# A NaN-ignoring row maximum: the first small tile becomes a group of its own

## The chip, the core and the metric

The kernel runs on one core of one Trainium2 chip. The metric is the device time of one execution in microseconds (us); the median of three runs is given. A core has several engines that work side by side and wait for one another through semaphores. Four are used here: DVE (vector engine), ACT (scalar engine), POOL (GpSimd) and SP, which only issues the transfers. Sixteen DMA engines carry out those transfers between HBM, the main memory, and SBUF, the on-chip memory with its 128 partitions.

## The reference

The input has 32 x 2048 = 65,536 rows of 2048 floats, with one value in ten NaN. For each row the largest value that is not NaN is wanted.

```python
def reference(x: np.ndarray, axis: int) -> np.ndarray:
    return np.nanmax(x, axis=axis).astype(np.float32)
```

The input is 536.87 MB, the output 0.26 MB. Every input byte is read once.

## The kernel before

**Groups and tiles.** The rows are cut into groups, and each group is spread over the 128 partitions: with s rows per partition, partition p holds the s rows from row p x s of the group on. In memory the step from one partition to the next is therefore s x 8 KB. L299 makes this view for the loads and L300 the same for the results. A group is worked through in tiles, each of them some rows of every partition. `TILES` (L16 on) lists 74 of them. Tile 0 has one row per partition (1 MB in all), each of tiles 1 to 73 has seven (7168 KB), so the tiles hold 512 rows per partition. `GROUPS` (L50) cuts the list into groups of 15, 15, 15, 15, 13 and 1 tiles, that is 99, 105, 105, 105, 91 and 7 rows per partition.

**One tile.** An entry of `TILES` has three lists in quarter rows (512 floats): how the tile is cut into loads, into pieces for ACT and POOL, and into reduces for DVE. Most tiles are one load of 56 KB per partition, three pieces and two reduces. The last dozen tiles are cut ever finer. Loads are issued on SP (L316). ACT then reads the upper 16 bits of each float and writes a 16-bit key in which every NaN has become a very low value (L235, written to one of three key buffers `kt`). POOL turns the key back into the upper half of a float, in place in the tile (L245); for a part of the pieces ACT does that instead. DVE takes the maximum of each row (L252).

**What sets the order.** The program writes its order out by hand. A small class, `Order`, gives each instruction the semaphore waits that it needs, and each engine carries out its instructions in the order in which they are written. There are three tile buffers `xt`: the load of a tile waits for the last reduce of the tile three before it. So at any time the queue of SP holds about two loads. All loads go through that one queue.

**Results.** The row maxima of groups 0 to 3 are gathered in a buffer `acc`, those of the last two in a part of a small buffer `lead`. `LATE` (L54) names the first group that goes to the second buffer. A row that has only NaN shows up as a particular very low value; two instructions over all maxima of a buffer (`find`, L258 and L272) look for it and turn it into NaN. `FLAGGED` (L53) says behind which groups DVE does so: behind group 3 for groups 0 to 3 together, and behind group 5 for that group. For group 4 POOL does it, as its last work. The stores of the results, one per group, are issued on SP behind the last load (L460 on); each waits for the check of its group.

Of the kernel before, what the change touches and what calls it, by code (L numbers as in the profile page):

```python
# [15 lines left out]
TILES = (  # L16
    [([4], [4], [4])]
    + [([28], [7, 9, 12], [16, 12])] * 7
    + [([28], [9, 12, -7], [8, 20])]
    + [([28], [7, 9, 12], [16, 12])] * 7  # L20
    + [([28], [9, 12, -7], [8, 20])]
    + [([28], [7, 9, 12], [16, 12])] * 7
    + [([28], [9, 12, -7], [8, 20])]
    + [([28], [7, 9, 12], [16, 12])] * 7
# [23 lines left out]
)  # L48

GROUPS = [TILES[i : i + 15] for i in range(0, 60, 15)] + [TILES[60:73], TILES[73:]]  # L50


FLAGGED = (3, 5)  # L53
LATE = 4  # L54

APART = (70, 71, 72, 73)
WIDE = 7
# [115 lines left out]
def kernel(  # L173
# [28 lines left out]
    of = out.bitcast(i32).flatten_outer_dims().rearrange("r c -> (r c)")  # L202
    rows = [sum(sum(loads) for loads, _, _ in g) * Q // D for g in GROUPS]
    assert R == P * sum(rows)
# [5 lines left out]

    early = sum(rows[:LATE])
    lead = sing.tile([P, LEAD // 4], f32, name="lead")
    acc1 = lead[:, : sum(rows[LATE:])]
    late = lead[:, LEAD // 4 - 1 - rows[LATE] : LEAD // 4 - 1].bitcast(i32)
    warm = lead[:, LEAD // 4 - 1 :]
# [5 lines left out]
    def maxima(lo, hi):  # L221

        if hi <= early:
            return acc0[:, lo:hi]
        assert lo >= early
        return acc1[:, lo - early : hi - early]

    with tc.tile_critical():  # L228
# [25 lines left out]
        def find(who, engine, deps, acc, none, op):  # L254
            e = order.add(
                who,
                engine,
                lambda: engine.tensor_scalar(  # L258
                    out=none,
                    in0=acc,  # L260
                    scalar1=NONE,
                    scalar2=float(0x00800000),
                    op0=ALU.is_equal,
                    op1=ALU.mult,
                ),
                deps,
            )
            bits = acc.bitcast(i32)
            return order.add(
                who,  # L270
                engine,
                lambda: engine.tensor_tensor(  # L272
                    out=bits, in0=bits, in1=none, op=op
                ),
                [e],
            )
# [20 lines left out]
        r0 = 0  # L297
        for gi, (s, g) in enumerate(zip(rows, GROUPS)):
            xg = xr[r0 : r0 + P * s].rearrange("(p s) d -> p (s d)", p=P)  # L299
# [144 lines left out]
            stores.append((og, acc.bitcast(i32)))  # L444
            if gi == LATE:
                late_after = after
            elif gi not in FLAGGED:
                continue
            lo, flagged = flagged, first + s
            if gi == LATE:  # L450
                late_acc = maxima(lo, flagged)
            else:
# [3 lines left out]
                ready += [e] * (gi + 1 - len(ready))  # L456
            if gi == len(GROUPS) - 1:
                e = find("pool", nc.gpsimd, late_after, late_acc, late, ALU.add)
                ready[LATE] = e
        for (og, bits), e in zip(stores, ready):  # L460
# [46 lines left out]
```

## Time and profile before

| | before |
|---|---|
| time, median of 3 runs | 1252.76 us (1252.72 to 1252.77) |
| span of the profiled execution | 1251.6 us |
| its own time beside the span | not given apart; the median is 1.2 us above the span |
| busy: DVE, ACT, POOL | 1110.8, 965.6, 1168.5 us |
| DMA, mean over the span | 429 GB/s |
| a load of one tile, issue to landing (median) | 22.6 us |

The span runs from the first to the last instruction on the core. A busy time is the sum of an engine's instructions. In the lines of the groups and the timeline, "out<-in" names the buffers, a number with "x" behind it counts instructions, and what stands in brackets is the idle time ahead of the instruction and what ended it. "SPq" is the queue on which SP issues transfers. Tiles are counted from 0 in this text.

### The profile page before, as it was taken

Reading aid. Unit: us, or ns where it says so; the run is one execution under the profiler, and the core shown is the slowest. Engines: PE = TensorE matmul, PEld = TensorE weight load, DVE = VectorE, ACT = ScalarE, POOL = GpSimd, SP = SyncE. Lnnn points to the kernel's source line nnn. Section 1 sums busy time; section 2 is a strip of 40 time slices with the busy share of each in tenths; the row PEclk is TensorE's granted clock in tenths of the full one; section 3 lists DMA queues with packets and bytes.
Section 4 is the critical chain, followed back from the end, with each engine's and each line's share of the span. In section 5 each row is a group of like instructions: output and inputs, shape, how many; then the busy total and the mean of one; then the engine's idle time right before and its main releaser. Section 6 shows DMA issues by size and latency. Waiting matters only on the chain.

```text
span 1251.6 us, 893 instructions
## 1 busy us (share of the span) xinstructions
DVE 1110.8 (89%) x181; ACT 965.6 (77%) x273; POOL 1168.5 (93%) x242
## 2 busy tenths in 40 slices
DVE  0888989888889888898988888988888899999999
ACT  3777887778777877788777877777777778999997
POOL 2999989998999899998999899999999999989998
DMA  9999999999999999999999999999999999999997
GB/s 415 440 411 440 440 433 418 440 440 440 431 420 440 440 438 431 422 440 440 438 433 420 440 440 438 434 418 440 440 438 435 420 438 436 425 438 429 429 427 299
DMA packets 15991, 537.20 MB, mean 429 GB/s; under 512 B 2544, under 2 KB 2544, under 8 KB 3568
## 3 DMA queue, kind: packets, MB, share of 16 engines
q1 hardware_dynamic: 15984, 537.14, 99.4%
q14 instruction: 7, 0.06, 0.0%
HBM read 536.87 MB, written 0.26 MB: 429 GB/s over the span
## 4 chain that ended last, share of the span: by engine, by line
DMA 40%; DVE 29%; POOL 21%; ACT 8%; issue 1%; SPq 0%
DMA xt<-in_x_dram 40%; DVE acc L252 21%; POOL xt L245 21%; ACT kt L235 8%; DVE lead L252 7%; ACT xt L235 1%; SPq L316 0%; DVE none L258 0%; DVE lead L272 0%; SPq L502 0%; SPq L228 0%
## 5 line engine op out<-in xcount | busy, mean ns | idle before, releaser
L245 POOL TENSOR_SCALAR xt<-kt 128x3584 int16<-128x3584 uint16 (+11 forms) x236 | 1167.4, 4946 | 78.3 <-ACT kt L235 64.9
L235 ACT ACTIVATE kt<-xt 128x3584 uint16<-128x3584 int16 (+9 forms) x247 | 913.4, 3734 | 278.7 <-DMA xt<-in_x_dram 258.6
L252 DVE TENSOR_REDUCE acc<-xt 128x3 f32<-128x6144 f32 (+3 forms) x119 | 896.2, 7570 | 136.1 <-POOL xt L245 128.6
L252 DVE TENSOR_REDUCE lead<-xt 128x1 f32<-128x2048 f32 (+4 forms) x56 | 211.4, 3848 | 1.0 <-POOL xt L245 0.9
L235 ACT ACTIVATE xt<-kt 128x512 int16<-128x512 uint16 (+6 forms) x24 | 52.9, 2204 | 0.7
L235 ACT ACT_TABLE_LOAD x1 | 1.3, 1283 | 0.9 <-SPq L228 0.9
L252 DVE TENSOR_REDUCE xt<-xt 128x1 f32<-128x1536 f32 x1 | 1.7, 1741 | 0.0
L278 DVE MEMSET lead<- 128x1 f32 x1 | 0.1, 59 | 1.0 <-SPq L228 1.0
L258 DVE TENSOR_SCALAR none<-acc 128x414 int32<-128x414 f32 x1 | 0.6, 592 | 0.0
L258 POOL TENSOR_SCALAR lead<-lead 128x91 int32<-128x91 f32 x1 | 0.5, 545 | 0.1
L272 DVE TENSOR_TENSOR acc<-acc,none 128x414 int32<-128x414 int32 x1 | 0.6, 586 | 0.0
L272 POOL TENSOR_TENSOR lead<-lead 128x91 int32<-128x91 int32 x1 | 0.4, 377 | 0.1
L488 POOL MEMSET const-float32-0.0<- 128x1 f32 x1 | 0.1, 98 | 0.2 <-issue 0.2
L235 ACT ACTIVATE lead<-lead 128x1 f32<-128x1 f32 x1 | 0.2, 203 | 0.0
L258 DVE TENSOR_SCALAR none<-lead 128x7 int32<-128x7 f32 x1 | 0.2, 169 | 0.0
L272 DVE TENSOR_TENSOR lead<-lead,none 128x7 int32<-128x7 int32 x1 | 0.2, 162 | 0.0
L488 POOL MEMSET const-bfloat16-1.0<- 128x1 bf16 x1 | 0.1, 101 | 0.0
L488 POOL MEMSET const-uint8-127<- 128x1 uint8 x1 | 0.1, 101 | 0.0
L488 POOL MEMSET const-float32-1.0<- 128x1 f32 x1 | 0.1, 98 | 0.0
## 6 DMA issues: line engine op xcount, KB each, us to landing
xt<-in_x_dram SPq DMA_DIRECT2D x61, 7168.0 KB, 22.6
xt<-in_x_dram SPq DMA_DIRECT2D x2, 5120.0 KB, 17.5
xt<-in_x_dram SPq DMA_DIRECT2D x3, 2816.0 KB, 22.7
xt<-in_x_dram SPq DMA_DIRECT2D x4, 2048.0 KB, 22.3
xt<-in_x_dram SPq DMA_DIRECT2D x5, 1536.0 KB, 29.1
xt<-in_x_dram SPq DMA_DIRECT2D x2, 3584.0 KB, 24.8
xt<-in_x_dram SPq DMA_DIRECT2D x6, 1024.0 KB, 26.8
xt<-in_x_dram SPq DMA_DIRECT2D x3, 1792.0 KB, 30.0
```

Of the source, the lines that this page charges most:

```text
L235: lambda: nc.scalar.activation(**kw),
L245: lambda: nc.gpsimd.tensor_scalar(**kw),
L252: return order.add("dve", nc.vector, lambda: do(**kw), deps)
L258: lambda: engine.tensor_scalar(out=none, in0=acc, scalar1=NONE, scalar2=float(0x00800000), op0=ALU.is_equal, op1=ALU.mult,),
L272: lambda: engine.tensor_tensor(out=bits, in0=bits, in1=none, op=op),
L278: e_warm = order.add("dve", nc.vector, lambda: nc.vector.memset(warm, 1.0), [])
L488: nc = _bacc.Bacc("TRN2", target_bir_lowering=False, num_devices=1)
```

## The change

Tile 0 becomes a group of its own, with one row per partition. Its source in memory is then one block of 1 MB. The other tiles are cut into groups of 15, 15, 15, 15, 12 and 1, that is 105, 105, 105, 105, 84 and 7 rows per partition. The order of the tiles and the lists of each tile stay as they are. There are seven groups for six, so the numbers in `FLAGGED` and `LATE` go up by one: DVE's check of the early groups now comes behind tile 60 and covers 421 maxima per partition (414 before), POOL's covers 84 (91 before), and there is one more store.

```diff
-GROUPS = [TILES[i : i + 15] for i in range(0, 60, 15)] + [TILES[60:73], TILES[73:]]
-
-
-FLAGGED = (3, 5)
-LATE = 4
+GROUPS = (
+    [TILES[:1]]
+    + [TILES[i : i + 15] for i in range(1, 61, 15)]
+    + [TILES[61:73], TILES[73:]]
+)
+
+
+FLAGGED = (4, 6)
+LATE = 5
```

## The prediction

> **What bounds the kernel now.** I read the page first: busy shares, the slices, the queues.
>
> ```profile
> DVE 1110.8 (89%) x181; ACT 965.6 (77%) x273; POOL 1168.5 (93%) x242
> ...
> DMA  9999999999999999999999999999999999999997
> ...
> q1 hardware_dynamic: 15984, 537.14, 99.4%
> ```
>
> Three engines are well used, but the DMA engines are busy in every slice but the last, and the one queue of SP takes 99.4% of the span. That the queue is also what the engines wait for is in the list of waits:
>
> ```profile
> ACT kt L235 <- DMA xt<-in_x_dram: 258.6, 69, 15.0
> DVE acc L252 <- POOL xt L245: 128.6, 57, 23.0
> POOL xt L245 <- ACT kt L235: 64.9, 68, 15.7
> ```
>
> Each engine waits for the one ahead of it, and ACT, the first, waits for loads. Next the span by stages (columns: length, busy time of DVE, ACT and POOL, clock, DMA share, GB/s), cut where the first packet of tiles 15, 30, 45 and 60 starts:
>
> ```profile
> 0.00:242.50 242.50, 187.37 (x27) 169.41 (x43) 210.05 (x43) 1.00 0.99 429
> 242.50:496.10 253.60, 226.56 (x31) 195.04 (x47) 239.50 (x44) 1.00 1.00 434
> 496.10:749.70 253.60, 227.18 (x31) 195.09 (x47) 240.22 (x44) 1.00 1.00 434
> 749.70:1003.40 253.70, 227.04 (x31) 186.12 (x45) 248.13 (x46) 1.00 1.00 434
> 1003.40:1224.00 220.60, 217.71 (x52) 198.91 (x73) 208.69 (x54) 1.00 1.00 431
> ```
>
> From tile 15 on, 15 tiles take 253.6 us, 16.91 us each, at 434 GB/s, whatever the group. The DMA packet records of the trace say the same: a packet is one partition's run; the 57,344-byte one takes 2116 ns, and eight of them per DMA engine are 16.93 us. The first load packet starts at 1.94 us and the last ends at 1242.6 us, with no hole between. So the time is a stream of 1240.7 us, 1.9 us ahead of it and 9.0 us behind it in the span of 1251.6 us; the 1.2 us from there to the median of 1252.76 us lie around the span, and I leave them.
>
> The sum may therefore change in four places: the pace of the packets, a hole in the stream, the 9 us behind it, and the start.
>
> **The pace of the packets.** Nothing is added to the bytes loaded; only the address step from one partition to the next changes: 99 rows of 8 KB to 1 (tile 0) or 105 (tiles 1 to 14), 105 or 91 to 84 for tiles 61 to 72, 105 to 105 elsewhere, save tile 60, which goes from a step of 91 to one of 105. I summed in the packet records by how much packets exceed the usual duration of their size. Tile 0: 128 packets of 8192 bytes take 2956 ns per DMA engine where 8 x 309 = 2472 are usual, 0.48 us too much. Tiles 2 to 11: 13.2 us over 16 engines, 0.82 us. Tiles 1 and 12 to 14 have none. From tile 15 to the end there are 1.5 us over 16 engines, 0.09 us, beside instruction fetches on the other queue. Together 1.4 us, all that pace can give back.
>
> For tile 0 the load of one block of 1 MB is not in the trace. Nearest rows: the 8192-byte loads of tile 73 (step of 7 rows), all at the usual 309 ns, give a gain of 0.48 us; the slowest packet of tile 0 now (1208 ns) for all eight gives (1208 x 8 - 2956) = 6.7 us lost. Tile 0 is nearest to itself: same size, same 16 engines starting together. So zero, and ends of -0.48 and +6.7 us (the upper one needs every packet as slow as the worst of 128).
>
> For tiles 1 to 14 the step becomes that of groups 1 to 3, which show no slow packets (gain 0.82 us); but tiles 1 and 12 to 14 show none at 99 either, so the slow spell looks like something of the first 190 us, and could as well double. I take zero, ends -0.82 and +0.82.
>
> For 84 rows, nothing in the trace has an even step. Three changes of step are in it, 99 to 105 at tile 15, 105 to 91 at tile 60 and 91 to 7 at tile 73, and the packet duration stays at 2116 ns through the first two and at the usual one of each size after the third. Zero; the lower end is zero too, since those packets already run at the usual duration; the upper end is the slowest tile of the trace, tile 10 (3.6 us over 16 engines, 0.23 us), for all 12 tiles: +2.7 us. The Trainium skill, page "DMA: Bandwidth & Descriptors", section "Latency and other measured facts", speaks against such a step: copies with a row pitch of 512 KiB ran at 207 GB/s against 214, and worse at 2 MiB and up. By it, estimated from that page's smallest loss, the 84-row step (672 KiB, not a power of two) would lose 3.3% of about 204 us, 6.7 us. No run here has such a pitch.
>
> **A hole in the stream.** A load is issued when the last reduce of the tile three before it has ended. Issue time and first packet give the lead: 26 us at tile 3, 4.9 us at tile 4, 3.40 us at the least (tile 60, issued at 999.99), then 5.3 us at tile 64 and 28 us near the end. An empty queue needs 1.00 us (tile 0). So 2.4 us of cover at the worst place. The check for empty rows over the early groups now comes after tile 60 instead of 59. Now it reads:
>
> ```profile
> 1018.14 15.14 DVE L252 TENSOR_REDUCE acc<-xt 128x4 f32<-128x8192 f32 x2 [1.80 <-POOL xt L245]
> 1033.32 0.59 DVE L258 TENSOR_SCALAR none<-acc 128x414 int32<-128x414 f32 x1
> 1033.95 0.59 DVE L272 TENSOR_TENSOR acc<-acc,none 128x414 int32<-128x414 int32 x1
> 1035.05 23.80 DVE L252 TENSOR_REDUCE lead<-xt 128x4 f32<-128x8192 f32 x4 [0.51 <-POOL xt L245]
> 1059.25 21.71 DVE L252 TENSOR_REDUCE lead<-xt 128x3 f32<-128x6144 f32 x3 [0.40 <-POOL xt L245]
> ```
>
> The two instructions lie in DVE's wait for POOL and cost nothing: after them 0.51 us are idle still. Moved to 1050.2, they stand between reduces that run back to back. With 421 columns for 414 they take 0.60 + 0.60 us, and with the gaps and the lost overlap of 0.08 us about 1.36 us. Behind them wait tile 61's two reduces, then the 0.40 + 0.08 us of slack at 1059.25; DVE goes on 0.87 us late. The load of tile 64 waits for tile 61, so its lead drops from 5.3 to 4.4 us: no hole. Later loads have 7 us and more. DVE wins the delay back in its small waits (0.09 at 1065.82, 0.14 at 1141.42, 0.05 at 1187, 0.45 at 1223.76, 0.30 at 1228.75 us; together 1.03). If that cover were gone, up to 0.87 us would go on to the end, but there stand 1.05 and 1.56 us more:
>
> ```profile
> 1237.55 5.54 DVE lead L252 x3
> 1243.08 1.05 issue
> 1244.13 0.64 DVE lead L252
> 1244.77 1.56 issue
> 1246.33 2.29 DVE lead L252
> ```
>
> Those waits are for POOL, which does not wait for DVE's reduces: its last stretch starts at 1204.68, when a load has landed. The term is zero, ends 0 and +0.87.
>
> **Behind the stream.** One more store is issued, 128 runs of 4 bytes. It stands behind the last load on SP, ahead of the stores of groups 1 to 4:
>
> ```profile
> 1222.61 9.02 SPq L464 DMA_DIRECT2D out_dram<-acc  x4
> 1247.23 2.13 SPq L464 DMA_DIRECT2D out_dram<-lead  x2
> ```
>
> Four issues end at 1231.6; a fifth at the dearest price of the four, 4.4 us, ends at 1236.0, 11.2 us before SP's next issue, which waits for POOL (15.6 us in the list of SP's waits). Nothing else is queued on SP. On the DMA engines it adds 8 packets each of some 7 ns (the 28-byte packets of the last store). The waits behind it stay: the final wait for stores counts one more, which landed long before. Zero; were all of it on the path, 0.06 us. POOL's check reads 84 columns for 91, at most 7/91 of 0.92 us = 0.07 us sooner, and its store goes out 1.8 us before the last one, which sets the end. Zero. Storing tile 60's maxima in the other buffer costs no instruction.
>
> **The start.** Same issue (0.38 us), same 1.00 us to the first packet. Tile 0 landing a little sooner or later moves ACT, POOL and DVE inside waits of 15 to 23 us for tile 1. Zero.
>
> Sum: 0 on a profiled execution of 1251.6 us of span, 1252.76 us by the median; I say 1252.7.
>
> **The rivals.**
>
> Slow packets go with the step of 99 rows, or with the strided first load. For it: only group 0 has them. Against: tiles 1 and 12 to 14. Gain 0.82 us, with tile 0's 0.48 up to 1.3: 1251.9 to 1251.5.
>
> The opposite: 1 MB in one block makes the 16 engines collide at the start, or the slow spell of the first tiles doubles. For it: tile 0 is slow at the start already. Against: tile 73's 8192-byte packets. Loss of 0.5 to 1.3 us: 1253.3 to 1254.1.
>
> The other side, slower: the step of 84 rows makes the packets of tiles 61 to 72 slow. At tile 10's pace 2.7 us: 1255.5. It decides from 0.21 us per tile on (2.5 us over 12 tiles). Against: the odd steps don't differ from each other. By the skill's page, at 6.7 us, the time would be 1259.5.
>
> The load of 1 MB does not spread over the 16 engines, because its source is one block. One engine would then carry 128 x 309 ns = 39.6 us instead of 2.5, and as later loads need all engines, about 37 us would be lost: 1290. Against: the store of the last group (128 x 28 bytes) has a destination in one block too, and is done in 0.20 us of packets, where one engine would need 128 x 7 ns = 0.9 us.
>
> **How the numbers follow.** No change to speak of (1252.2 to 1253.2): 0.58. Slow packets gone: 0.18. More of them at the start: 0.15. Slow step of 84: 0.06. Load on few engines: 0.01. Anything else: 0.02, half to each side. All of the first three lie within 0.2% (2.5 us, about what a measurement of this kernel can tell from no change): same 0.91, slower 0.08, faster 0.01. Range: all 1.4 us of slow packets gone, 1251.4, to as much again, 1254.1; it holds the first three cases, 0.91, as their bounds demand.
>
> **What would show it.** Right: a stream from 1.9 to 1242.6 us, stages of 15 tiles in 253.6 us, the 84-row stage still at 16.9 us a tile; the check at about 1050 us, the next DVE waits shorter, the last POOL stretch at the same time; five early stores done before 1237. Wrong: a DMA share under 1.00 or a lower GB/s between 1020 and 1224, tile 1 starting on ACT later than 22.64 us by more than 1 us, or SP's last two stores waiting for something other than POOL and DVE.

## The result: 3.3 us slower

The changed kernel takes 1256.08 us (median of 7 runs, 1255.23 to 1257.31) against 1252.76 us before (1252.45 to 1253.11): a ratio of 1.0026, 95% interval [1.0017, 1.0036]. The forecast was 1252.7 us with a range up to 1254.1 us. Two small things that it had priced at zero are the loss: the added store of 128 runs of 4 bytes, some 3.0 us, and the check of empty rows moved by one tile, 0.3 to 0.5 us.

The profiled run is the fastest of the seven (1255.23 us), with a span of 1253.4 us. In all runs that list both, the time is 1.7 to 1.8 us above its own span, not 1.2. So the profiled execution before, with its span of 1251.6 us, took about 1253.4 us (an estimate), 0.6 us above the median. That is why the two profiles differ by 1.8 us only, where the medians differ by 3.32 us. The stages, in the columns of the table before:

```profile
242.50:496.10 253.60, 226.46 (x31) 195.05 (x47) 239.50 (x44) 1.00 1.00 434
496.10:749.70 253.60, 227.19 (x31) 195.07 (x47) 240.30 (x44) 1.00 1.00 434
749.70:1003.40 253.70, 226.95 (x31) 186.12 (x45) 248.11 (x46) 1.00 1.00 434
```

These are the stages before to a tenth of a microsecond. By the packet records the stream of loads even ends earlier, at 1242.20 us (1242.62 before); that is no gain of the change, since the stream of b_plus28 below, with the old groups, ends at 1241.99 us. All of the difference lies behind it. The chain that ended last:

```profile
1221.71 23.93 DMA xt<-in_x_dram
1245.64 0.02 issue
1245.67 1.06 ACT kt L239
1246.73 0.07 issue
1246.80 1.34 POOL xt L249
1248.14 0.02 issue
1248.17 2.30 DVE lead L256
```

The last load is issued at 1221.71 us and lands at 1245.64 us, 3.4 us after its last packet. Before, it landed at 1243.02 us, 0.4 us after. ACT waits for it, POOL for ACT, and DVE's last reduce starts at 1248.17 instead of 1246.33 us: 1.84 us, which is the difference of the spans. ACT's and DVE's lines in the timeline say the same, first those before:

```profile
1243.58 1.55 ACT L235 ACTIVATE kt<-xt 128x1024 uint16<-128x1024 int16 x2
```

```profile
1223.76 24.84 DVE L252 TENSOR_REDUCE lead<-xt 128x1 f32<-128x513 f32 x12
```

The same lines in the changed kernel:

```profile
1245.67 1.57 ACT L239 ACTIVATE kt<-xt 128x1024 uint16<-128x1024 int16 x2 [2.39 <-DMA xt<-in_x_dram]
```

```profile
1223.77 22.62 DVE L256 TENSOR_REDUCE lead<-xt 128x1 f32<-128x513 f32 x11
1248.17 2.29 DVE L256 TENSOR_REDUCE lead<-xt 128x1 f32<-128x2048 f32 x1 [1.78 <-POOL xt L249]
```

A transfer has landed when all 16 DMA engines have counted up its semaphore. For the last load twelve had done so by 1241.61 us. The other four, which finish last, did so at 1243.39, 1244.71, 1245.23 and 1245.64 us. In that time the new store's writes are under way: nearly all their packets take 9 ns, but its counts come in between 1241.5 and 1247 us. (All stores count up one semaphore, and the counts bear no names; here and below they are put down to the stores in their order.)

### The profile page after: what moved, and what is told of

It reads as the page before. It is cut to its first block, busy times and chain, and to the rows that moved or that the text cites. A ratio compares the mean times of both kernels' runs of the same rounds, so it can differ in the third digit from the quotient of the medians.

```text
span 1253.4 us, 894 instructions
## 1 busy us (share of the span) xinstructions
DVE 1110.6 (89%) x181; ACT 965.8 (77%) x273; POOL 1169.0 (93%) x242
## 4 chain that ended last, share of the span: by engine, by line
DMA 37%; DVE 35%; POOL 16%; ACT 9%; SPq 2%; issue 1%
DMA xt<-in_x_dram 37%; DVE acc L256 23%; POOL xt L249 16%; DVE lead L256 12%; ACT kt L239 8%; SPq L320 2%; ACT xt L239 1%; DVE none L262 0%; DVE acc L276 0%; DVE lead L276 0%; SPq L506 0%; SPq L232 0%
## 5 line engine op out<-in xcount | busy, mean ns | idle before, releaser
L256 DVE TENSOR_REDUCE acc<-xt 128x3 f32<-128x6144 f32 (+3 forms) x121 | 911.4, 7571 | 137.3 <-POOL xt L249 130.0
L256 DVE TENSOR_REDUCE lead<-xt 128x1 f32<-128x2048 f32 (+4 forms) x54 | 196.0, 3708 | 1.8 <-POOL xt L249 1.8
```

The source lines that it names most:

```text
L256: return order.add("dve", nc.vector, lambda: do(**kw), deps)
```

## The experiments

The theory after the result: the writes of the 4-byte store take microseconds and hold up other transfers, and nothing else in the change costs much. The rivals: the new steps between partitions; the moved check; any additional small store. Differences are against runs of the kernel before beside them on the same chip. The intervals of the ratios are about 0.1% (1.1 us) to each side, so for less than that I also give the spread of the runs.

| run | median us | before beside it | difference | ratio, 95% interval |
|---|---|---|---|---|
| a_again (the changed kernel) | 1257.07 | 1252.89 | +4.18 | 1.0032 [1.0021, 1.0044] |
| a_no0 | 1253.29 | 1252.98 | +0.31 | 1.0002 [0.9993, 1.0011] |
| a_behind | 1255.18 | 1252.98 | +2.20 | 1.0017 [1.0008, 1.0026] |
| a_wait | 1255.65 | 1252.76 | +2.89 | 1.0022 [1.0013, 1.0031] |
| a_elsewhere | 1253.98 | 1252.90 | +1.08 | 1.0010 [1.0000, 1.0019] |
| a_elsewhere2 | 1254.19 | 1252.89 | +1.30 | 1.0011 [1.0001, 1.0020] |
| a_early | 1271.11 | 1252.90 | +18.21 | 1.0146 [1.0132, 1.0160] |
| a_early3 | 1258.38 | 1252.76 | +5.62 | 1.0045 [1.0030, 1.0061] |
| a_8rows | 1253.26 | 1252.90 | +0.36 | 1.0004 [0.9995, 1.0013] |
| a_8rows_2checks | 1252.88 | 1252.76 | +0.12 | 1.0002 [0.9993, 1.0010] |
| b_check60 | 1253.36 | 1252.90 | +0.46 | 1.0003 [0.9995, 1.0012] |
| b_plus4 | 1253.75 | 1252.98 | +0.77 | 1.0006 [0.9997, 1.0015] |
| b_space16 | 1253.62 | 1252.89 | +0.73 | 1.0005 [0.9996, 1.0015] |
| b_space64 | 1252.92 | 1252.89 | +0.03 | 1.0000 [0.9990, 1.0009] |
| b_plus28 | 1253.07 | 1252.98 | +0.09 | 1.0000 [0.9991, 1.0009] |
| b_split4 | 1252.69 | 1252.76 | -0.07 | 0.9999 [0.9990, 1.0008] |

**Without the store (a_no0).**

```diff
-        for (og, bits), e in zip(stores, ready):
+        for (og, bits), e in list(zip(stores, ready))[1:]:
```

> The changed kernel without the store of group 0 (the first 128 row maxima are computed and not written). If the 4-byte store is the whole loss: the last load lands about 0.5 us after its last packet, near 1242.7 us, as before (it landed at 1245.6 with 1242.2 for the last packet), and the time is 1252.3 to 1252.8 us. If the new steps between partitions, the block load or the moved check of empty rows cost something, the time stays 1255 to 1256 us and the late landing stays.

+0.31 us; its runs (1253.20 to 1253.37) all lie above those of before (1252.82 to 1253.13). That is above the 1252.3 to 1252.8 us expected, but on this chip the kernel before takes 1252.98 us itself. The last load lands at 1242.80 us, as expected. So the store is nearly the whole loss, and the new steps, the block load, the moved check and the seven groups together cost some 0.3 us. What the 0.3 us are is asked further down.

**Its place in the queue (a_behind, a_wait).** In the first the store is issued behind the four other early stores; in the second it waits there, besides, until the last load has landed.

```diff
+        both = list(zip(stores, ready))
+        for (og, bits), e in both[1:5] + both[:1] + both[5:]:
```

> The changed kernel with group 0's store issued behind the stores of groups 1 to 4, nothing left out. If the store only hurts because its packets follow the last load directly: the last load lands near 1242.7 us, the 4-byte store about 5 us after its packets start, near 1248 us, still before the last store, and the time is 1252.3 to 1253.0 us. If one store more, wherever it stands, costs its time: 1255 to 1256 us as the changed kernel.

> The changed kernel with the 4-byte store issued behind the stores of groups 1 to 4 and only once the last load has landed. Then no load can be held up by it: the last load lands near 1242.7 us and the compute ends 0.4 us later than before (the moved check). The store's own 6 to 8 us from about 1243 us run into the last two stores: they land near 1251 us instead of 1250.4. Sum 0.8 to 1.5 us above before, against 2.2 us (behind the four stores) and 3.3 us (the changed kernel). If the late landing of the load was not the main loss: 2 us or more.

In both, the first alternative missed and the time fell into the range of the second. Behind four stores the load still lands late, at 1244.99 us, and +2.2 us remain. With the wait the load lands at 1242.32 us and DVE ends at 1248.8 us, 0.2 us earlier than in the profile before. Yet the time is +2.9 us, since now the last two stores land late. SP's list of waits in that run (what is waited for, us in total, times, longest us):

```profile
SPq L508 <- DMA out_dram<-lead: 2.9, 1, 2.9
```

That is the wait at the end for the last store, 0.5 us before. The last store (3.5 KB) took 3.9 us from issue to landing instead of 1.4, though it was issued at 1248.8 us and the 4-byte store had landed, by the order of the counts, at 1248.3 us, 6.0 us after its issue. Which of the stores was late is not shown, since they share the semaphore. Shown is that the stores are done only 10 us after the 4-byte store was issued. So the late load is one way in which that store costs time, and not the only one: what is to land in those microseconds pays.

**Ahead of loads (a_early, a_early3).** DVE checks group 0 right behind tile 0, and its store is issued then.

> The changed kernel with group 0 checked by DVE right behind tile 0 and its 4-byte store issued then, ahead of tile 3's load; the check of groups 1 to 4 stays behind tile 60. If the store only costs what follows it in the tail: a late landing of tile 2 or 3 by up to 4 us near 40 us that the lead of 5 us swallows, and 0.3 to 0.5 us above before at the end (the moved check). If the store costs its time wherever it stands: 2 us or more above before.

The expectation says "ahead of tile 3's load", but as SP issues in the written order the store stood ahead of tile 1's. That alone made a hole: tile 1's first packet starts at 14.4 us instead of 5.1 us in the changed kernel. The rest is the price of the writes, behind which the packets of tile 1 start 0.4 us later. The store in the list of DMA issues (KB, us from issue to landing):

```profile
out_dram<-acc SPq DMA_DIRECT2D x1, 0.5 KB, 8.3
```

Its 128 packets start between 13.80 and 13.99 us and take 7 to 9 ns each; the store lands at 21.30 us. If the writes went one by one, that is 7.3 us / 128 = 57 ns each (an estimate; in a_wait, with no load left, it is 4.9 us or 39 ns, by the order of the counts). And the first packet of tile 1 on each of the 16 DMA engines takes 7.9 to 11.6 us instead of 2.1. The excess of tile 1's packets is 135 us over 16 engines, 8.5 us; with the hole of 9.3 us and the check of 0.4 us that makes the 18.2 us measured.

The second run puts the store where it was meant to be, ahead of tile 3's load:

```diff
+                if number == 3:
+                    order.add("sp", nc.sync, lambda: nc.sync.dma_start(out=og0, in_=bits0),
+                              [e0], lane="store", step=16)
```

> As the kernel with the early store, but the store stands ahead of tile 3's load (in the run before it stood ahead of tile 1's load, so that the stream stood still for 9 us). If the 4-byte writes hold up what follows on each DMA engine: the packets of tile 3 that start behind them take some 10 us instead of 2.1, the stream loses 6 to 8 us for good, 1259 to 1262 us. If the lead of 26 us of tile 3's load covers it: 0.4 to 0.6 us above before.

ACT's timeline, one pair of lines for each tile:

```profile
39.88 7.12 ACT L239 ACTIVATE kt<-xt 128x3584 uint16<-128x3584 int16 x2 [4.22 <-DMA xt<-in_x_dram]
47.38 5.32 ACT L239 ACTIVATE kt<-xt 128x6144 uint16<-128x6144 int16 x1 [0.37 <-POOL xt L249]
61.95 7.12 ACT L239 ACTIVATE kt<-xt 128x3584 uint16<-128x3584 int16 x2 [9.25 <-DMA xt<-in_x_dram]
```

Tile 3 comes 22.1 us after tile 2 instead of 17.0. Its packets exceed the usual by 75 us over 16 engines, 4.7 us, less than the 6 to 8 expected, and the time is up by 5.6 us. A lead of 26 us does not help: packets on the DMA engines themselves are held up (up to 6.7 us each), and a stream without a hole does not get that back.

**What makes the writes slow (b_plus4, b_plus28, b_split4, b_space16, b_space64).** The kernel before gets one more store of 128 runs right behind the last load; in b_split4 the first column of group 0's own store is split off.

```diff
+        extra = order.add("sp", nc.sync,
+            lambda: nc.sync.dma_start(out=tail, in_=acc0[:, :1].bitcast(i32)),
+            [ready[0]], lane="extra", step=16)
```

> The kernel before with one more store of 128 x 4 bytes into one block of 512 bytes, right behind the last load (into the place of the last group's results, which are stored over it at the end). If the 4-byte store is the cause: 1255 to 1257 us and the last load lands 2 us or more late. If the groups' new steps are the cause: 1252.7 to 1252.9 us.

> The same with 128 x 28 bytes into one block of 3584 bytes. If runs of 4 bytes into one small block are slow, and not any small store behind the last load: landing of the last load within 0.5 us of before, 1252.7 to 1253.2 us. If any store below some hundred bytes does it: 1255 to 1257 us.

> The kernel before with the store of group 0 in two: first the first row of each partition (128 runs of 4 bytes, 396 bytes apart, over 50 KB), then the other 98 rows. If runs of 4 bytes are slow wherever they go: as with the block, 0.7 us or more above before, the 4-byte store landing 5 us or more after its packets. If it is that many engines write into one block of 512 bytes: within 0.2 us of before, the store landing within 1.5 us of its packets.

> The kernel before with one more store of 128 x 4 bytes, 16 bytes apart (2 KB in all), right behind the last load. If the cost comes from many short writes into few bytes of memory, it lies between the block of 512 bytes (store landed 6 us late, 0.8 us above before) and the spread of 396 bytes (nothing): landing 1 to 4 us after its packets, 0.1 to 0.6 us above before. If only writes that touch each other are slow: nothing.

> The same 64 bytes apart (8 KB in all). If the unit is a line of up to 64 bytes that several engines write: nothing, as at 396 bytes. If the unit is a block of 512 bytes or more: still 1 us or more from packets to landing.

The added store in the lists of DMA issues, first of b_plus4 (runs that touch), then of b_space16, then of b_space64; all three are issued between 1222.0 and 1222.4 us:

```profile
out_dram<-acc SPq DMA_DIRECT2D x1, 0.5 KB, 25.8
```

```profile
out_dram<-acc SPq DMA_DIRECT2D x1, 0.5 KB, 22.3
```

```profile
out_dram<-acc SPq DMA_DIRECT2D x1, 0.5 KB, 21.1
```

With 128 runs of 28 bytes that touch it is 21.5 us (landing at 1243.50), with 4 bytes 396 bytes apart 19.6 us (landing at 1241.59). The times follow, with three surprises. The first is b_plus4, which missed both of its alternatives: all its runs (1253.36 to 1254.09) lie above those of before (1252.82 to 1253.13), but only by 0.8 us. Its last load lands on time, at 1242.7 us, and the loss is in the last stores (the last one takes 2.0 us instead of 1.4). Another is b_split4: 4-byte runs as such cost nothing. The third is that runs of 28 bytes in a row cost nothing either, nor 32 bytes (a_8rows, below).

So it takes both: runs of a few bytes, and several of them close together. At a distance of 4 bytes (16 runs to 64 bytes) the store is slow, at 64 and 396 it is not. At 16 bytes (four runs to 64) it is slow by a little: 1.2 us longer than at 64 bytes, and the last load lands 1.36 us after its last packet, where the runs without such writes have 0.3 to 0.7 us; the time is up by 0.73 us, but its runs (1253.00 to 1253.96) overlap those of before (1252.74 to 1253.22). The place of the block changes with the distance, but is not what decides: in the middle of the output, where the stores of 16 and 64 bytes went, touching runs are slow as well (27.3 us in a_elsewhere2, below). As for the length, three or four runs of 28 bytes to 64 bytes are not slow.

That such writes go one after another fits all of these runs, but is not shown; which stretch of memory is the unit, and where between 4 and 28 bytes a run becomes long enough, was not tried. The Trainium skill, page "DMA: Bandwidth & Descriptors", section "Specifications", says that below 512 bytes a DMA engine reads, changes and writes back. The runs agree that short writes can be dear and add that length alone does not decide.

**Its place in memory (a_again, a_elsewhere, a_elsewhere2).** In the kernel before the added block cost 0.8 us, in the changed kernel nearly 3. So its store was sent to two other blocks of 512 bytes, where results are stored over it later.

> The changed kernel once more, on the chip of the next three runs. 2.5 to 4 us above before, the last load landing at 1244.5 us or later, if the late landing belongs to this kernel; if it belonged to one chip, 0.8 to 1.3 us as with the store sent elsewhere.

> The changed kernel with the 4-byte store sent to another block of 512 bytes, near the end of the output (stored over later by the last group; the first 128 results are not written). If the place matters, and it is why the added store in the kernel before cost 0.8 us only: the last load lands near 1242.8 us and the time is 0.8 to 1.3 us above before. If only size and position in the queue matter: 2 to 3.5 us above before, and the last load lands at 1244.5 us or later.

> The changed kernel with the 4-byte store sent to a block of 512 bytes in the middle of the output, where group 5's results are stored over it later (the first 128 results are not written). If the start of the output is special: 0.8 to 1.5 us above before and the last load on time, as with the block near the end. If the place is chance: anything from 0.8 to 3.5 us. The store of group 5 waits for this one, which lands near 1247.5 us, so up to 0.5 us more is possible.

In both other places the last load lands on time (1242.74 and 1242.41 us), and 1.1 and 1.3 us remain: the moved check, and later landings of the last stores. Part of the 1.3 us is made by the experiment: SP waits 2.8 us for the 4-byte store there before it issues the last two. In a_again, which with +4.18 us is just above its expected 2.5 to 4, the load lands at 1248.13 us:

```profile
1221.62 26.50 DMA xt<-in_x_dram
1248.13 0.02 issue
1248.15 1.06 ACT kt L239
```

The two profiles of the changed kernel are of its fastest and its slowest run, 1255.23 and 1257.72 us, and the landings of the last load differ by the same 2.49 us. So the late landing is what sets the loss of the changed kernel. It goes with the store as the change has it, but not for certain with its place: in both runs with another place, and in b_plus4, the store also counts up a semaphore of its own, where in the changed kernel it shares that of the other stores. The two were not tried apart, and in b_space16 a load landed 1 us late in another place. What holds back the load stays open.

**The moved check (b_check60, a_8rows, a_8rows_2checks).** The first moves the check alone, in the kernel before. The second joins tiles 0 and 1 into one group, so that the runs have 32 bytes (the diff without its last two lines). The third splits the check besides.

```diff
-    [TILES[:1]]
-    + [TILES[i : i + 15] for i in range(1, 61, 15)]
+    [TILES[:2], TILES[2:16]]
+    + [TILES[i : i + 15] for i in range(16, 61, 15)]
...
-FLAGGED = (4, 6)
+FLAGGED = (3, 4, 6)
```

> The kernel before with one thing alone: DVE's check of the early groups (414 maxima) stands behind tile 60 instead of tile 59. If DVE has no idle time left from 1059 us to the end (the waits that the prediction counted on being only the time until the reduce before had ended), the check's 1.36 us less the 0.5 us idle ahead of tile 61's last reduce and some 0.4 us of true idle later come out at the end: 0.3 to 0.5 us slower than before. If the waits in the tail are real, as the prediction had it: 0.0 to 0.1 us.

> The changed kernel with tile 1 put into the first group too (groups of 8, 98, 105, 105, 105, 84 and 7 rows): the same number of groups and stores, but the first store has 128 runs of 32 bytes into 4 KB. If the 4-byte runs are the cause: the last load lands within 0.8 us of its last packet, as without the store, and the time is 0.3 to 0.5 us above before. If one more small store near the start of the output is: 2 us or more above before.

> The changed kernel with groups of 8, 98, 105, 105, 105, 84 and 7 rows, and DVE's check in two: 316 maxima behind tile 45, where DVE waits for POOL, and 105 behind tile 60. If the moved check is what is left of the loss once the 4-byte runs are gone: the part behind tile 60 shrinks from 1.36 to about 0.7 us, most of which the 0.5 us of idle covers, and the time is 0.0 to 0.2 us above before (0.36 with one check). If the new steps between partitions cost it: 0.3 to 0.4 us again.

+0.46 us with the check alone (1253.20 to 1253.47; 26 of the 27 runs before lie at 1253.11 or below, one at 1253.29), +0.36 us with 32-byte runs, +0.12 us with two checks. Only the first is nearly clear of the runs before. The profiles are clearer. From the end of the last load packet to the start of DVE's last reduce it is 3.71 us before (3.68 to 3.75 in b_plus28, b_split4 and b_space64), 4.11 in b_check60, 4.09 in a_no0 and 4.06 in a_8rows, but 3.72 with two checks. So the check behind tile 60 costs 0.35 to 0.4 us at the end, and a check of 105 columns there costs nothing. DVE's timeline in b_check60:

```profile
1034.60 15.15 DVE L252 TENSOR_REDUCE lead<-xt 128x4 f32<-128x8192 f32 x2 [1.74 <-POOL xt L245]
1049.78 0.59 DVE L258 TENSOR_SCALAR none<-acc 128x414 int32<-128x414 f32 x1
1050.41 0.59 DVE L272 TENSOR_TENSOR acc<-acc,none 128x414 int32<-128x414 int32 x1
1050.91 30.25 DVE L252 TENSOR_REDUCE lead<-xt 128x2 f32<-128x4096 f32 x5
```

The wait for POOL ahead of tile 60, 0.5 us long when the check filled it, is 1.74 us now and unused. Behind the check there is no wait any more where 0.40 us stood. DVE then runs without a pause. In a_no0, whose tail is not disturbed, POOL's last piece for it ends at 1245.61 us and DVE's last reduce starts only at 1246.18 us, when the reduce before has ended. Before, it started 0.2 us after POOL's last piece, and there too the reduce before was only just ending (at 1246.41 us; reduces that follow each other directly overlap by 0.08 us). So the end hung on DVE already, and what delays DVE in this stretch comes out at the end.

None of these kernels is clearly below the kernel before. Nothing in the change gains what its store and check cost.

## Why the prediction was wrong

**Behind the stream: the step that failed.** "8 packets each of some 7 ns ... were all of it on the path, 0.06 us." The packets do take 7 to 9 ns. But a packet's duration is evidently not that of its write. The writes took 7.3 us to land in a_early, and around them loads (a_early), other stores (a_wait) and the counts of a load (the changed kernel) came late. The nearest row that I took, 28-byte runs in one block, seemed near; b_plus28 shows that such a store is free, so nothing could be read from it. The row that would have warned is not in the trace before; with no row for it, the upper end should not have been 0.06 us. Measured: 4.18 - 0.31 = 3.9 us (a_again against a_no0, on two chips) and 3.32 - 0.31 = 3.0 us.

"The final wait for stores counts one more, which landed long before" holds in the changed kernel: the store lands near 1247 us, the last one at 1252.3 us, and the final wait is 0.5 us as before. The loss came out elsewhere: "it stands behind the last load" was to make the store harmless, and it is that load's landing that came late.

**A hole in the stream: the second step that failed.** The check was costed about right: 1.36 us on DVE, where it moved the next reduce by 1.26 us (from 1049.68, the end of the reduce ahead less the usual overlap, to 1050.94 us). But "DVE wins the delay back", and "there stand 1.05 and 1.56 us more", were wrong. Those "issue" pieces in the chain are not idle time: they run from a short instruction, with which DVE's queue takes a semaphore wait early, to the next reduce, and the reduce before is still at work (1241.94 to 1244.22 us). Of the 1.03 us of small waits, the 0.45 us at 1223.76 and the 0.30 us at 1228.75 us are none either: the reduces ahead of them end at 1223.73 and 1228.83 us. The row that tells it is the last one of the stage table before, with DVE busy 24.93 us between 1224.0 us and its last instruction at 1249.0 us:

```profile
1224.00:1251.60 27.60, 24.93 (x14) 21.07 (x19) 21.88 (x16) 1.00 0.70 284
```

The list of waits before has no wait of DVE there either. Its two waits for POOL are the 0.51 and 0.40 us behind the check:

```profile
DVE lead L252 <- POOL xt L245: 0.9, 2, 0.5
```

The term was 0.3 to 0.5 us, inside its ends of 0 and 0.87.

**The pace of the packets: right in the sum.** The slow spell is a matter of the execution, not of the 99-row step: b_plus28 has that step, and tiles 2 to 11 exceed the usual by 0.04 us there instead of 0.82; the changed kernel by 0.08, and a_8rows_2checks, without that step, by 1.1. So the rival "slow packets go with the step of 99 rows" falls, and its gain would have been small in any case: the streams of the changed kernel and of a_no0 end 0.4 and 0.5 us earlier than in the profile before, and a_no0 is still not faster. Tile 0 as one block starts at 1.96 us and ends at 5.47 us (5.42 before): its term was zero, as taken.

**The step of 84 rows: right.** From tile 60 on the packets exceed the usual by 0.3 us over 16 engines in either kernel, and with that step a_8rows_2checks is 0.12 us above before. The rival of 1255.5 us came near the measured time by luck, since what it rests on did not happen. The loss that the prediction worked out from the Trainium skill, page "DMA: Bandwidth & Descriptors", section "Latency and other measured facts", was for large powers of two; at 672 KiB no run here shows one.

**The start: right,** and so is POOL's check (0.50 + 0.36 us, before 0.55 + 0.38). The load of one block is not left to few engines: its 128 packets are done in 3.5 us, as before.

No rival named a store that lands late. Of the chance of 0.08 for slower, 0.07 went to mechanisms that did not happen and 0.01 to anything else; the case that did happen was priced at 0.06 us at the most.

## What to carry to other kernels

Beware of a store of one value per partition into consecutive words: it cost 0.8 us in the mildest case here (b_plus4), some 3 us in the changed kernel, and most ahead of a load. Give such a group more values per partition (runs of 28 or 32 bytes cost nothing here), or, where the layout allows it, store them spread out (64 bytes or more apart). And take an engine's slack from the sum of its busy times in a stage or from its list of waits, not from "issue" pieces of the chain.

## What was unexpected of the hardware

- 128 writes of 4 bytes into 512 bytes land 7.3 us after the last of their packets has started (a_early), though the packets last 7 to 9 ns; the same writes 64 bytes apart or more cost no time that was measured.
- Around them other transfers come late: a 57,344-byte packet of the next load took up to 11.6 us instead of 2.1 (a_early), a 420-byte packet 2.5 us instead of 0.025 (a_again), and a store of 3.5 KB landed after 3.9 us instead of 1.4 (a_wait).
- In the changed kernel the landing of a load came 3.4 and 6.0 us after its last packet (0.3 to 0.7 us without such a store). With the store in another place and on a semaphore of its own it did not. The cause is open.
